# An S5 layer's tail on one core: gate stored raw, states copied by ScalarE, differences of four rows on GpSimd

## The chip, the core and the metric

One of the cores of a Trainium2 chip runs the whole kernel. TensorE (PE) does the matrix products, VectorE (DVE), ScalarE (ACT) and GpSimd (POOL) the elementwise work, and SyncE (SP) and ScalarE issue the transfers between HBM and the on-chip memory SBUF; products land in PSUM. Each engine works through its own list of instructions in a fixed order and waits on semaphores of the others. The metric is the device time of one execution in microseconds (us).

## What is computed

The reference is an encoder trunk of four layers, two with latent attention and two with an S5 state-space layer. The change touches the S5 layer, in short:

```python
u     = x @ w_u                        # 64 groups of 16 channels
s     = scan(lam, B u)                 # complex diagonal recurrence along the sequence
y     = gelu(C s + D u + ...)          # outputs of the groups, width 1024
gate  = silu(x @ w_gate)
o     = (y * sigmoid(y @ w_glu + b_glu) * gate) @ w_out
x     = layer_norm(ALPHA * x + o)
```

All of it is float32; a product is made of three matrix products of rounded parts (a high part and the difference that is left).

## The kernel before, in words

The 1536 tokens (1024 of the prompt, 512 of the sample) lie along the free dimension, the 1024 channels are eight rows of 128 partitions (row m, or kt when it is the inner dimension of a product). `mm3` (L89, L90, L91) multiplies: high by high, high weight by row difference, weight difference by high.

The S5 layer runs in overlapping stages. `states_in` (L1235 to L1239) brings the inputs of the states of eight groups at a time from PSUM to two SBUF places, SA for the first half of the groups and SB for the second. `step` (L1249, L1250) is one step of the scan on VectorE, for one of two sequences (128 and 64 chunks) of one half; `advance` deals such steps out among other work. `gate` makes passes over `x @ w_gate` on TensorE with weights streamed from HBM (WG); the last six are passes 8 to 13, two columns of 512 tokens each. At a pass's end ScalarE writes silu of each product to a buffer in R (L1356) and from there to HBM (SG2).

Between the matrix products of passes 8 to 13 come `first(0)` to `first(9)`. Each calls `states_out(i)` (L1376 on VectorE, L1377 and L1378 on ScalarE), which turns the states of four groups into the order that the next product reads and puts them in one place in X0/X3 (for i from 10 on, two places by turns), and `outputs(i)` (L1392 to L1394 on TensorE, Gelu L1396 on ScalarE), whose result goes to HBM as Y. Outputs 0 to 7 need the scan of the first half, 8 to 15 that of the second.

Then comes the glu product `y @ w_glu`. `load_y(m)` fetches a row of Y (L1438), GpSimd rounds it to the high part (L1439), VectorE takes the difference (L1440). `load_w(m)` does the same for weights (L1453 load, L1454 on ScalarE, L1455 on VectorE). Rows 0 and 1 go to X2, which the operand of the gate product holds until the last pass is done; rows 2 to 5 go to SA, which is free once the states of output 7 are copied. Weights 0 go to XN, weights 1 to X1. `early(kt)` makes the part of row kt of six products at once (six accumulators of the first two output rows), in between outputs 10 to 15. `finish` (L1468, L1471, L1473, L1474) adds the two parts of y on VectorE, multiplies by the gate on GpSimd, takes the sigmoid of the product on ScalarE, multiplies on VectorE and stores. It is called 24 times.

Names: S and B are PSUM tiles; SA, SB, XN, R and X0 to X3 are regions of SBUF (X in the profile is any of the last four). The program is written in one order and a scheduler with a timeline of its own sets the fixed order of each engine's list.

## Time and profile before

| | us |
|---|---|
| median of 3 runs (lowest, highest) | 1635.17 (1633.77, 1637.13) |
| profiled execution, whole | 1637.0 |
| its span, first to last instruction | 1635.1 |
| PE busy | 1569.0 (96%) |
| DVE busy | 1113.1 (68%) |
| ACT busy | 584.6 (36%) |
| POOL busy | 307.7 (19%) |

The mean granted clock of TensorE is 0.986 of full speed. To read the profile: the share of busy time tells which engine is close to its limit overall; the table of waits tells on what TensorE stood still and how long; the table of stretches tells where its clock fell; and the rows of time tell which instruction on which engine ended a wait.

### The profile page before, as it was taken

How to read it: one execution, taken by the hardware profiler on the slowest of the kernel's cores; microseconds unless marked ns; L12 is line 12 of the kernel's file. 1: busy time of each engine (PE TensorE's matmuls, PEld its weight loads, DVE VectorE, ACT ScalarE, POOL GpSimd, SP SyncE). 2: the span in 40 equal slices, each digit the busy share in tenths (PEclk: the TensorE clock that was granted, in tenths of full speed). 3: DMA queues.
4: the chain of work that ended last, by engine and by line, in shares of the span. 5: the costliest groups of instructions: out<-in, count | busy, mean ns of one | idle time of the engine just before them, and what ended most of it. 6: DMA issues, size and time to landing. Idle time of an engine off the chain costs nothing.

```text
span 1635.1 us, 23610 instructions
## 1 busy us (share of the span) xinstructions
PE 1569.0 (96%) x7948; PEld 1330.2 (81%) x7948; DVE 1113.1 (68%) x3077; ACT 584.6 (36%) x1025; POOL 307.7 (19%) x524
## 2 busy tenths in 40 slices
PE   7999999899999999999999999999899969999997
PEld 7997878788888888788888888887678758888886
DVE  5549992667776766888667742499489863554766
ACT  3434331344535444444511113416625425321000
POOL 6810000322223222343201000000000001333110
PEclk9999999999999999999999999999999979999999
DMA  5665566523222335533434427525687738765443
GB/s 185 170 174 188 174 224 227 169 74 90 62 81 87 103 98 172 180 105 101 156 125 130 132 74 189 159 40 155 186 255 240 238 122 253 230 193 185 146 146 89
DMA packets 205928, 249.66 MB, mean 153 GB/s; under 512 B 26608, under 2 KB 149104, under 8 KB 204784
## 3 DMA queue, kind: packets, MB, share of 16 engines
q1 hardware_dynamic: 197168, 232.36, 47.3%
q10 hardware_dynamic: 8640, 15.80, 2.6%
q8 instruction: 63, 1.03, 0.3%
q14 instruction: 57, 0.47, 0.1%
HBM read 155.89 MB, written 90.11 MB: 150 GB/s over the span
## 4 chain that ended last, share of the span: by engine, by line
PE 75%; DMA 9%; DVE 7%; ACT 3%; SPq 2%; issue 2%; POOL 1%; ACTq 0%; DVEq 0%; POOLq 0%
PE B L90 12%; PE B L89 12%; PE B L91 12%; PE S L89 8%; PE S L91 8%; PE S L90 8%; PE B L554 3%; PE S L1230 2%; PE S L520 2%; PE S L519 2%; DMA SA<-CH 1%; PE B L1393 1%; PE B L1394 1%; DMA SG<-R 1%; DMA R<-WG 1%
## 5 line engine op out<-in xcount | busy, mean ns | idle before, releaser
L89 PE MATMUL B<-X,SB 128*128 128x512 f32 x392 | 155.2, 396 | 0.0
L90 PE MATMUL B<-X,SB 128*128 128x512 f32 x392 | 154.1, 393 | 0.0
L91 PE MATMUL B<-X,SB 128*128 128x512 f32 x392 | 153.9, 393 | 0.0
L539 POOL TENSOR_SCALAR SC<-SC,R 128x1024 f32<-128x1024 f32 (+1 forms) x96 | 98.5, 1027 | 214.2 <-DVE R L538 189.7
L556 ACT CAST X<-B 128x512 fp32r<-128x512 f32 x160 | 89.5, 591 | 129.0 <-PE B L554 128.4
L557 DVE TENSOR_TENSOR X<-B,X 128x512 fp32r<-128x512 f32 x160 | 105.8, 683 | 25.3 <-ACT X L556 25.0
L532 ACT ACTIVATE SC<-S,R 128x1024 f32<-128x1024 f32 (+1 forms) x96 | 93.9, 978 | 62.9 <-DVE R L529 54.0
L529 DVE TENSOR_REDUCE R<-S 128x1 f32<-128x1024 f32 (+1 forms) x96 | 99.3, 1039 | 24.0 <-PE S L520 23.9
L554 PE MATMUL B<-ident,SC 128*128 128x128 f32 x640 | 88.7, 272 | 2.0 <-POOL SC L539 2.0
L554 PEld LDWEIGHTS B<-ident,SC 128*128 128x128 f32 x640 | 76.2, 140 | 16.2 <-POOL SC L539 2.5
L89 PE MATMUL B<-X,R 128*128 128x512 f32 x192 | 80.1, 418 | 6.7 <-DMA R<-WG 3.7
L91 PEld LDWEIGHTS B<-X,SB 128*128 128x128 f32 x392 | 74.0, 189 | 15.3
L89 PEld LDWEIGHTS B<-X,SB 128*128 128x128 f32 x392 | 74.0, 189 | 14.7
L90 PEld LDWEIGHTS B<-X,SB 128*128 128x128 f32 x392 | 74.0, 189 | 14.7
L1250 DVE TENSOR_TENSOR SB<-SB,scan 128x32 f32<-128x32 f32 (+1 forms) x504 | 80.0, 209 | 0.2 <-DMA R<-WG 0.2
L1250 DVE TENSOR_TENSOR SA<-SA,scan 128x32 f32<-128x32 f32 (+1 forms) x504 | 78.2, 212 | 0.0
L90 PE MATMUL B<-X,R 128*128 128x512 f32 x192 | 76.5, 398 | 0.0
L91 PE MATMUL B<-X,R 128*128 128x512 f32 x192 | 75.9, 395 | 0.0
L89 PE MATMUL S<-SA,X 128*128 128x384 f32 (+2 forms) x200 | 68.6, 347 | 5.7 <-POOL SA L96 5.5
L1249 DVE TENSOR_TENSOR scan<-SB,lam 128x64 f32<-128x64 f32 (+1 forms) x252 | 57.3, 260 | 21.2 <-ACT SB L1238 21.2
L90 PE MATMUL S<-SA,X 128*128 128x384 f32 (+2 forms) x200 | 68.0, 342 | 0.3 <-DVE SA L97 0.3
L91 PE MATMUL S<-SA,X 128*128 128x384 f32 (+2 forms) x200 | 68.0, 341 | 0.0
(461 smaller groups left out, 4206.7 us busy)
## 6 DMA issues: line engine op xcount, KB each, us to landing
R<-WG SPq DMA_DIRECT2D x112, 128.0 KB, 3.5
R<-EU SPq DMA_DIRECT2D x52, 224.0 KB, 3.2
EU<-SA SPq DMA_DIRECT2D x16, 512.0 KB, 3.6
WO<-SA SPq DMA_DIRECT2D x8, 1024.0 KB, 5.3
WG<-X SPq DMA_DIRECT2D x16, 512.0 KB, 3.0
X<-WO SPq DMA_DIRECT2D x16, 512.0 KB, 6.0
SG<-SC ACTq DMA_DIRECT2D x24, 256.0 KB, 3.1
SC<-SG SPq DMA_DIRECT2D x24, 256.0 KB, 2.9
```

What stands on the lines that cost most here:

```text
L89: nc.tensor.matmul(ps, ah, bh, start=first, stop=False)
L90: nc.tensor.matmul(ps, ah, bl, start=False, stop=False)
L91: nc.tensor.matmul(ps, al, bh, start=False, stop=last)
L519: nc.tensor.matmul(S[:, cs], qs[:, q], self.kr[kc][0], start=False, stop=False)
L529: nc.vector.reduce_max(nm, self.S[:, :L], axis=AX.X, negate=True)
L532: nc.scalar.activation(P, self.S[:, :L], AF.Exp, bias=nm, accum_out=rsum)
L539: nc.gpsimd.tensor_scalar(P, P, rsum, 0.0, op0=ALU.mult, op1=ALU.add)
L554: nc.tensor.transpose(ps[:, t, :], P[:, (t0 + t) * 128:(t0 + t + 1) * 128], self.k.ident)
L556: nc.scalar.copy(a[:, :, qsl], ps)
L557: nc.vector.tensor_sub(b[:, :, qsl], ps, a[:, :, qsl])
L1249: return [lambda: nc.vector.tensor_mul(t, prev.unsqueeze(2).broadcast_to(sh), lam), lambda: nc.vector.tensor_add(cur, cur, t[:, 0]), lambd ...
L1250: lambda: nc.vector.tensor_add(cur, cur, t[:, 0]), lambda: nc.vector.tensor_add(cur, cur, t[:, 1])]
```

## The change

The diff, cut to its core (line numbers of the changed kernel are one or two lower than those of the kernel before up to about L1425, and one to five higher from there to L1476):

```diff
-    nc.scalar.activation(k.bcol[:, 0:1], sg[:, 0:1], AF.Exp, scale=0.0)
...
     a.kproj(0, 1)
+    k.nc.scalar.activation(k.bcol[:, 0:1], k.gq[:, 0:1], AF.Exp, scale=0.0)
...
-    yield
-    nc.vector.tensor_scalar(s1, k1, 127.0, 8388608.0, op0=ALU.add, op1=ALU.mult)
-    nc.vector.tensor_scalar(s2, kf, 127.0, 8388608.0, op0=ALU.add, op1=ALU.mult)
+    nc.gpsimd.tensor_scalar(s1, k1, 127.0, 8388608.0, op0=ALU.add, op1=ALU.mult)
+    nc.gpsimd.tensor_scalar(s2, kf, 127.0, 8388608.0, op0=ALU.add, op1=ALU.mult)
...
-                k.xn = Region(k, "XN", (8, F32R), (4, F32))
+                k.xn = Region(k, "XN", (10, F32))
...
-            nc.scalar.activation(sg, acc[c], AF.Silu)
+            nc.scalar.copy(sg, acc[c])
...
     def states_out(i):
-        reg, at = (xb, 9) if i >= N0 and i % 2 == 0 else (xa, 25)
+        reg, at = ((k.xn, 0), (xa, 25))[i % 2]
...
-        nc.vector.tensor_copy(st[0:64], xv[0:64])
+        nc.scalar.copy(st[0:64], xv[0:64])
...
-    yat = {0: (xc, 0), 1: (xc, 12)}
+    sy = Region(k, "SA", (48, F32R))
+    yat = {m: (sy, 12 * m) for m in range(4)}
+    yat.update({4: (xc, 0), 5: (xc, 12)})
...
-        nc.vector.tensor_sub(y[:, 1], raw, y[:, 0])
+        (nc.gpsimd if m < 4 else nc.vector).tensor_sub(y[:, 1], raw, y[:, 0])
...
-        if m:
-            reg, at = gat[m % 3]
-        else:
-            reg, at = k.xn, 0
+        reg, at = gat[m % 3]
...
-            reg, at = (xb, 22 if m < 3 else (16, 12)[m % 2] + 2 * h) if m else (k.xn, 8 + 2 * h)
+            reg, at = (xb, 22 if m < 3 else (16, 12)[m % 2] + 2 * h) if m else (k.xn, 6 + 2 * h)
...
-        nc.gpsimd.tensor_mul(sg, sg, y)
         sig = xb.tile([128, 512], F32, "fsig", 8, 10, 20)
         nc.scalar.activation(sig, ps, AF.Sigmoid, bias=bcol[:, m:m + 1])
+        t = k.xn.tile([128, 512], F32, "ft", 0, 2, 4)
+        nc.scalar.activation(t, sg, AF.Sigmoid)
+        nc.vector.tensor_mul(y, y, t)
+        nc.gpsimd.tensor_mul(sg, sg, y)
```

In words: the gate's products go to HBM as they are, and `finish` makes silu of them as the product with a sigmoid, one more instruction on ScalarE and one more on VectorE in each of 24 calls. `states_out` is wholly on ScalarE, with two places by turns for all sixteen outputs. Rows 0 to 3 of y lie in SA and their differences are taken by GpSimd; rows 4 and 5 lie in X2. Weights 0 of the glu go to X2 and no longer to XN, whose place holds states (their raw parts stay in XN). An instruction that makes ScalarE hold the table for Exp moves from the end of the first phase to the start of attention, and four small integer instructions move from VectorE to GpSimd.

What this does to the order on two engines is shown below. The first piece is ScalarE's list at outputs 8 to 10 in the kernel before; SB is the place of the second half's states, B the outputs' PSUM tiles (L1377 and L1378 are copies of states, L1396 the Gelu of an output):

```order
L1377 COPY X3_10778<-SB_9622 64x8x128
L1377 COPY X1_11903<-SB_9622 64x8x128
L1396 ACT_TABLE_LOAD
L1396 ACTIVATE X0_10777<-B_11820 128x384
L1396 ACTIVATE X0_10777<-B_11828 128x384
L1377 COPY X3_10778<-SB_9622 64x8x128
L1378 COPY X3_10778<-SB_9622 64x8x64
L1396 ACTIVATE X0_10777<-B_11872 128x384
```

The same place in the changed kernel, from the last copy of a gate product (L1355) on; L1453 is the rounding of glu weights, XN_8528 and X3_10777 the two places of states:

```order
L1355 COPY R_8539<-B_11795 128x512
L1453 CAST X2_11904<-XN_8528 128x512 x2
L1453 CAST X1_11903<-X1_11902 128x512
L1356 DMA SG2_66<-R_8539 128x512
L1453 CAST X1_11903<-X1_11902 128x512
L1375 COPY XN_8528<-SB_9621 64x1536
L1376 COPY XN_8528<-SB_9621 64x8x128
L1375 COPY X3_10777<-SB_9621 64x1536
L1376 COPY X3_10777<-SB_9621 64x8x128
L1395 ACTIVATE X0_10776<-B_11819 128x384
L1395 ACTIVATE X0_10776<-B_11827 128x384
L1375 COPY XN_8528<-SB_9621 64x1536
```

The copies of the lower 64 partitions (L1375; on VectorE before, L1376 there) stand ahead of the others on ScalarE, the table load is gone, and all four roundings of weights 0 and 1 stand between the last gate product and the first copy. The next piece is VectorE's list near the end of the second half's scan in the kernel before; SB and scan2 are the scan's operands, L1440 the difference of a row of y, L1455 that of weights:

```order
L1440 TENSOR_TENSOR X2_11905<-X2_11905 128x1536
L1250 TENSOR_TENSOR SB_9622<-SB_9622,scan2_81 128x2x16 x2
L1249 TENSOR_TENSOR scan2_81<-SB_9622,lam_78 128x4x16 x2
L1250 TENSOR_TENSOR SB_9622<-SB_9622,scan2_81 128x2x16 x4
L1249 TENSOR_TENSOR scan2_81<-SB_9622,lam_78 128x4x16
L1440 TENSOR_TENSOR X2_11905<-X2_11905 128x1536
```

And near the end of that scan in the changed kernel (L1248 and L1249 are the scan's steps there, L1454 the weights' difference):

```order
L1248 TENSOR_TENSOR scan2_81<-SB_9621,lam_78 128x4x16 x2
L1454 TENSOR_TENSOR X2_11904<-XN_8528,X2_11904 128x512
L1249 TENSOR_TENSOR SB_9621<-SB_9621,scan2_81 128x2x16 x2
L1454 TENSOR_TENSOR X2_11904<-XN_8528,X2_11904 128x512
L1249 TENSOR_TENSOR SB_9621<-SB_9621,scan2_81 128x2x16 x2
L1454 TENSOR_TENSOR X1_11903<-X1_11902,X1_11903 128x512
```

Before, four differences of rows of y and two of weights 1 stand among the scan's last instructions. Now all four differences of weights stand there instead: two and two scan instructions lie between the first three, 29 between the third and the fourth, and 7 behind it, so that 40 scan instructions follow the first. The rows' four differences stand on GpSimd, each behind a rounding.

TensorE's list holds the same instructions in both kernels from the last gate product to the last instruction of output 15 (90 products 128x512 and 94 pairs 128x192), in a slightly different order.

## Rows read from the trace of the kernel before

**Rows 1.** What TensorE waited for, 1200 to 1430 us: total, count, longest.

```profile
PE S L89 <- POOL X L1439: 6.5, 1, 6.5
PE B L1393 <- ACT X L1377: 3.9, 1, 3.9
PE B L1393 <- ACT X L1378: 3.5, 1, 3.5
PE B L89 <- DMA R<-WG: 2.4, 2, 2.0
```

**Rows 2.** Stretches: busy PE, PEld, DVE, ACT, POOL (instructions), granted clock, DMA share, GB/s.

```profile
1300.00:1325.00 25.00, 16.36 (x51) 12.01 (x52) 22.00 (x115) 3.52 (x5) 5.20 (x3) 0.73 0.59 201
1325.00:1350.00 25.00, 17.64 (x71) 16.22 (x70) 12.14 (x59) 10.66 (x10) 0.00 (x0) 0.80 0.18 56
...
1425.00:1450.00 25.00, 25.00 (x112) 20.71 (x111) 15.69 (x18) 4.74 (x7) 10.36 (x7) 1.00 0.67 202
```

**Rows 3.** Rows of time, TensorE: start, duration; gate's end (next product waits), end of output 15.

```profile
1308.14 0.59 PE L1392 MATMUL B<-X 128*128 128x192 f32 x2 [1.15 <-ACT R L1356]
1315.24 0.79 PE L89 MATMUL S<-X,XN 128*128 128x512 f32 x1 [6.51 <-POOL X L1439]
...
1384.53 0.49 PE L1393 MATMUL B<-X,X 128*128 128x192 f32 x2
1384.85 0.49 PE L1394 MATMUL B<-X,X 128*128 128x192 f32 x2
```

**Rows 4.** Rows of time, VectorE: start of the second half's scan, first copies behind it.

```profile
1174.56 0.29 DVE L1249 TENSOR_TENSOR scan<-SB,lam 128x128 f32<-128x128 f32 x1 [21.17 <-ACT SB L1238]
...
1331.54 2.84 DVE L1376 COPY X<-SB 64x1536 f32<-64x1536 f32 x2
```

**Rows 5.** VectorE's groups beside the scan, 1174.5 to 1332: busy, mean ns, idle before.

```profile
L1376 DVE COPY X<-SA 64x1536 f32<-64x1536 f32 x8 | 12.4, 1552 | 6.3 <-PE B L1394 6.3
L1440 DVE TENSOR_TENSOR X<-X 128x1536 fp32r<-128x1536 f32 x2 | 3.5, 1754 | 2.0 <-POOL X L1439 2.0
L1440 DVE TENSOR_TENSOR SA<-SA 128x1536 fp32r<-128x1536 f32 x2 | 3.5, 1753 | 4.9 <-POOL SA L1439 4.9
L1455 DVE TENSOR_TENSOR X<-X,X 128x512 fp32r<-128x512 f32 x2 | 1.4, 688 | 1.0 <-ACT X L1454 1.0
```

**Rows 6.** Groups of ScalarE, 1330 to 1375 us; the last over the whole span.

```profile
L1377 ACT COPY X<-SB 64x1024 f32<-64x1024 f32 x8 | 15.6, 1963 | 12.5 <-DVE SB L1250 12.3
L1378 ACT COPY X<-SB 64x512 f32<-64x512 f32 x6 | 6.5, 1079 | 0.0
L1396 ACT ACTIVATE X<-B 128x384 f32<-128x384 f32 x13 | 6.2, 490 | 13.5 <-PE B L1394 13.4
...
L1278 ACT CAST SB<-SC 128x1024 fp32r<-128x1024 f32 x8 | 8.5, 1057 | 16.7 <-PE B L90 9.9 <-DMA SC<-in_w_u 5.7 <-PE B L91 1.0
```

**Rows 7.** Rows of time of GpSimd, then VectorE, where both work.

```profile
1304.35 1.48 POOL L1439 TENSOR_SCALAR SA<-SA 128x1536 fp32r<-128x1536 f32 x1 [11.81 <-DMA SA<-Y]
...
1303.67 0.35 DVE L1249 TENSOR_TENSOR scan<-SB,lam 128x64 f32<-128x64 f32 x2
...
1304.40 1.64 DVE L1249 TENSOR_TENSOR scan<-SB,lam 128x64 f32<-128x64 f32 x2
...
1316.89 1.55 DVE L1250 TENSOR_TENSOR SB<-SB,scan 128x32 f32<-128x32 f32 x2
```

**Rows 8.** Groups of GpSimd and VectorE in the finish stage.

```profile
L1471 POOL TENSOR_TENSOR X<-X 128x512 f32<-128x512 f32 x24 | 35.5, 1482 | 69.4 <-DMA X<-SG 69.3
...
L1474 DVE TENSOR_TENSOR X<-X 128x512 f32<-128x512 f32 x24 | 23.3, 975 | 12.5 <-POOL X L1471 11.5 <-ACT X L1473 1.0
```

**Rows 9.** DMA issues: count, KB each, median us to landing; 1405 to 1540, then 1300 to 1330.

```profile
X<-SG SPq DMA_DIRECT2D x22, 256.0 KB, 3.5
...
X<-in_w_glu SPq DMA_DIRECT2D x3, 256.0 KB, 2.5
```

**Rows 10.** The chain that ended last, at the start of attention.

```profile
292.63 1.28 ACT L315
```

More of the change, by code (lines that the diff above doesn't have):

```diff
@@ L1002, in prep_a @@
         step = ld["st"]
-        yield from exp_exact(self.k, self, step, step)
+        exp_exact(self.k, self, step, step)
         yield
@@ L1008, in prep_a @@
         cs = self.t("cs", [128, G])
-        yield from exp_exact(self.k, self, x, x)
+        exp_exact(self.k, self, x, x)
         yield
@@ L1490, in early @@
                 glu(acc[i][c], ws[i], kt, c)
-    def second_y():
-        sy = Region(k, "SA", (48, F32R))
-        yat.update({i: (sy, 12 * i - 24) for i in range(2, 6)})
     done = 0
-    second_y()
     for i in range(N0, 16):
```

## The prediction

> **What bounds the kernel now.** By the table of busy times TensorE is the busiest engine by far, so a change pays where it stands still or runs at half clock, and nowhere else. I read its waits first, for the stages that the change touches, then the stretches, then the rows of time around the longest waits. From 1200 to 1430 us there is one bad place: the glu's first product waits 6.5 us for row 0 of y, then two outputs wait 3.9 and 3.5 us for state copies [rows 1]. The stretches from 1300 and from 1325 hold only 16.36 and 17.64 us of TensorE work in 25, at a granted clock of 0.73 and 0.80; from 1425 TensorE has 25.00 of 25 [rows 2]. So after about 1400 the finish stage hides all that other engines do, and what can be gained in the S5 layer lies between the gate's end (about 1306.4: the first output product behind it starts at 1308.14 after a wait of 1.15) and the end of output 15 (1384.85 plus 0.33, so 1385.2) [rows 3].
>
> TensorE's work there is the same in both kernels: 90 products at 0.223 us (25.00 us for 112 [rows 2]) and 94 pairs at 0.325 (1384.53 to 1384.85 [rows 3]), 50.6 us in all. Before it takes 1385.2 - 1306.4 = 78.8 us, so 28 us at most are to be had. What sets the end of output 15 is a chain of two legs: the last step of the second half's scan (VectorE is through at 1331.5 [rows 4]), then the copies of states 8 to 15 and their outputs, 1385.2 - 1331.5 = 53.7 us.
>
> **First leg, the scan.** From 1174.56, when the second half may start, to 1331.54 VectorE has 157.0 us [rows 4]. Beside the scan it does 8 copies of states (12.4), 4 differences of y rows (3.5 + 3.5), 2 of weights (1.4), and it stands 6.3 + 2.0 + 4.9 + 1.0 = 14.2 us [rows 5]. That leaves 122.0 of scan. The change takes the copies, the rows and the waits ahead of them away. It puts the four weight differences into the last 40 scan instructions (order, VectorE). Six such instructions take 0.73 us (a round that begins at 1303.67, the next at 1304.40 [rows 7]), 40 take 4.8; so the first weight difference could come at 1174.6 + 122.0 - 4.8 = 1291.8.
>
> Against that stands GpSimd. While it rounded a row of y for 1.48 us at 1304.35, two scan instructions of VectorE took 1.64 instead of 0.35, and the like at 1316.89 (1.55) [rows 7]: while one works, the other stands. The change puts 4 differences of 128x1536 on GpSimd, which the trace doesn't have. From above: a product of 128x512 on GpSimd takes 1.48 with such disturbance in it [rows 8], three 4.4; from below, VectorE's own 1.75 [rows 5]. GpSimd's row is the nearer; I take 3.8. Four rows at 1.48 + 3.8 are 21.1 us in which VectorE stands, less 1.3 + 1.2 which the 122.0 hold already: 1291.8 + 18.6 = 1310.4. (The Trainium skill, GPSIMD Engine Reference, Performance versus the Vector engine, gives 4497 ns for a two-input add of 2048 columns, so an estimate of 3.4 for 1536; with it this leg would be 1.6 us shorter. No run shown so far has such an instruction.)
>
> The weights 0 now lie in X2, free only at the gate's end; I put that at 1305, since the outputs' copies ahead of it no longer wait for VectorE but the loads of three rows of y can still hold up the gate's weights as before (2.4 us [rows 1]). The rounding on ScalarE (0.6 each, between the 0.49 of 384 columns and the 1.06 of 1024 [rows 6]) is done by 1306.5, ahead of VectorE. Then: difference 0.69, scan 0.25, 0.69, 0.25, 0.69, at 1313.0. The last piece of weights 1 reuses the place of the one before: load 2.5 [rows 9], rounding 0.6, difference 0.69, 1316.8, while 29 scan instructions (3.5) go by; 7 more (0.85) end the scan at about **1318**, 13.5 us sooner than now. TensorE has its first 48 products (10.7 us) from 1311 on, to 1322.
>
> **Second leg, the state copies.** Per state ScalarE copied 64x1024 (1.96) and 64x512 (1.08) [rows 6]; it gets 64x1536 as well, which VectorE did in 1.55 [rows 5]. By the slope of the first two, 0.88 per 512, it takes 2.84 on ScalarE. That row is the right one, since it reads the same strided states; a plain rounding of 128x1024 takes 1.06 [rows 6], half of it. States 8 and 9 have their third piece done beforehand: 4.8 each. Then come, in ScalarE's order, six times two Gelus (0.98) and a whole state (5.88): 6.86. The last output takes TensorE 3.9. From the scan's end: 9.6 + 41.2 + 3.9 = 54.7, against 53.7 now. TensorE alone would need 1322 + 40 = 1362 for the rest, so this chain decides, at 1318 + 54.7 = 1372.7. Small overlaps of ScalarE's instructions and some half clock in TensorE's gaps I let cancel. Gain: 1385.2 - 1372.7 = **12.5 us**. Behind output 15 the same row loads and products follow; what TensorE does there stays.
>
> (The Trainium skill, ScalarE: Activation LUTs, What ACT_TABLE_LOAD costs, has one element a cycle, 186 ns + 0.833 per element: an estimate of 1.47 for 1536 columns. The rows of 64x1024 contradict it for these strided reads: 1.96 where it gives 1.04. By the page the time would be that of the first rival.)
>
> **The other parts.** In the gate passes ten table loads (Silu and Gelu by turns) of 1.28 each, as in [rows 10], go from ScalarE, 12.8 us; eight more copies (states 0 to 7) cost it 22.7. Two places let it work one output ahead there, with some 11 us of gate products in between, so I cost this at nothing; without that cover each state would cost a few us. In the finish stage each of 24 calls gains a sigmoid (0.6 to 0.7, as a rounding) and a product on VectorE (0.69 to 0.98 [rows 5, 8]) under 24 products of TensorE (5.36): nothing, with VectorE at 15.69 and ScalarE at 4.74 of 25 [rows 2]. At the start of attention the table load of 1.28 stands in the chain [rows 10]; moved to where ScalarE waits anyway, it gives 0 to 1.4, I take 1.0. The integer instructions are small and in the background: nothing.
>
> Sum: 1637.0 - 12.5 - 1.0 = 1623.5 for the profiled execution; the median lay 1.8 below it, so 1622.
>
> **Rivals.** (1) The forward copy runs on ScalarE at the plain rate: (1.057 - 0.490)/640 per column [rows 6], 1.5 for 1536. Then 2 x 3.5 + 6 x 5.5 + 3.9 = 44; TensorE and the chain meet at 1362, the gain is 23 + 1, time 1611. For it: forward reads, where those shown are reversed. Against it: the stride is the same. (2) GpSimd keeps VectorE from the scan longer. Each us of a difference beyond 3.8 costs four; at 6.9 the scan ends at 1330.4 and nearly all is lost: 1634, and 1630 at 6.0. For it: in the finish stage VectorE's product of 128x512 takes 0.98 on average beside GpSimd's, where 0.69 is plain [rows 5, 8]. (The Trainium skill, SBUF - State Buffer, SBUF: two separate sides, says that of a two-input instruction of VectorE and one of GpSimd the one that starts first blocks the other fully; the rows of 1.64 and 1.55 agree.) (3) Slower: the longer chain of a finish. Its gate buffer is one of two, so load, ScalarE, VectorE, GpSimd, VectorE must go round in two finishes, 10.7 us. Before: 3.5 [rows 9] + 1.48 + 0.98 = 6.0; now + 0.69 + 1.0 = 7.7, without time in each engine's queue. If the queues add more than 3.0 it decides; at 13 us each of some 18 finishes loses 1.15, 21 us in all: 1643. For it: GpSimd there already waits 69.3 us for gate loads [rows 8]. Against it: 3 us of queues each time is much for engines with a third idle.
>
> **How the numbers follow.** The forecast has 0.58, rival (1) 0.15, (2) 0.14, (3) 0.10, and 0.03 go to small losses in the gate passes. The forecast's own width, from the difference's bounds (1.75 to 4.4: -8 to +2.4 us, the low end cut off by loads at about -4) and 2 us each for gate's end and clock, is 1615 to 1629. The range takes in (1) and (2): 1609 to 1636, leaving out (3) and a little. A measurement of this kernel can tell about 0.2% or 3.3 us from no change. Faster: the forecast, (1) and half of (2), 0.80; same: half of (2) and the rest, 0.10; slower: (3), 0.10.
>
> **What would show it.** Right, if the scan's last step comes near 1318, the 64x1536 copy on ScalarE takes 2.6 to 3.0, ScalarE is busy without a gap from there to the last state, TensorE's waits there read "ACT L1375 to L1377" and the wait for the y row is gone; and if the stretches past 1400 still have TensorE at 25 of 25. Wrong, if the copy takes 1.5, if the GpSimd difference takes 6 or more, if TensorE waits for the weights' difference beyond 1312, or if a finish shows TensorE waiting on PSUM.

## The result, and the profile of the changed kernel

The changed kernel takes 1626.62 us (median of 6 runs, 1622.02 to 1628.78) against 1636.24 (6 runs, 1633.77 to 1637.36) for the kernel before beside it: a ratio of 0.9934 with a 95% interval of 0.9921 to 0.9946, so 10.8 us faster, with 8.8 to 12.9 by the interval. (The ratio is estimated from all the runs; the medians alone differ by 9.6 us.) The prediction said 1622, and a profiled execution 13.5 us below that of before; it is 12.4 below (1624.55 against 1637.0), and 12.3 by the spans (1622.8 against 1635.1). The size is close. How it is made up is not what the prediction said, and most of this part is about that.

The head of the page of the changed kernel, busy time by engine:

```profile
span 1622.8 us, 23654 instructions
PE 1565.0 (96%) x7948; PEld 1324.9 (82%) x7948; DVE 1104.4 (68%) x3077; ACT 633.2 (39%) x1056; POOL 322.7 (20%) x532
```

ScalarE has 49 us more than before and GpSimd 15, VectorE 9 less. None of that tells the time; TensorE's waits from 1200 to 1430 us do (us in total, times, longest), to be laid beside [rows 1]:

```profile
PE B L89 <- DMA R<-WG: 5.3, 2, 3.1
PE B L1392 <- ACT XN L1377: 4.8, 2, 2.5
PE B L1392 <- ACT XN L1376: 3.6, 1, 3.6
PE B L89 <- ACT R L1355: 1.1, 1, 1.1
```

The 6.5 us for row 0 of y are gone. The waits for copies of states are there as foreseen, and a bit larger. The loads of the gate's weights (WG) hold TensorE 5.3 us where it was 2.4. The stretches of 25 us that answer to [rows 2] (busy time of PE, PEld, DVE, ACT, POOL with counts, granted clock, DMA share, GB/s):

```profile
1300.00:1325.00 25.00, 20.34 (x80) 16.74 (x79) 7.83 (x44) 13.95 (x13) 2.95 (x1) 0.86 0.35 113
1325.00:1350.00 25.00, 19.37 (x93) 18.15 (x92) 1.76 (x1) 24.76 (x18) 1.47 (x1) 0.86 0.91 273
1425.00:1450.00 25.00, 25.00 (x112) 20.71 (x111) 14.42 (x20) 10.43 (x15) 6.84 (x5) 1.00 0.68 216
```

TensorE does 20.3 and 19.4 of 25 us where it did 16.4 and 17.6, at a clock of 0.86 for 0.73 and 0.80; from 1325 on ScalarE is at 24.76 of 25, the bound there. In the finish stage TensorE still has 25 of 25.

### The profile page after: what moved, and what is told of

It is laid out like the page before. It is cut to its first block, busy times and chain, and to the rows that moved or that the text cites. A ratio compares the mean times of both kernels' runs of the same rounds, so it can differ in the third digit from the quotient of the medians.

```text
span 1622.8 us, 23654 instructions
## 1 busy us (share of the span) xinstructions
PE 1565.0 (96%) x7948; PEld 1324.9 (82%) x7948; DVE 1104.4 (68%) x3077; ACT 633.2 (39%) x1056; POOL 322.7 (20%) x532
## 4 chain that ended last, share of the span: by engine, by line
PE 67%; DVE 12%; DMA 10%; ACT 5%; issue 2%; SPq 2%; POOL 1%; ACTq 0%; DVEq 0%; POOLq 0%
PE B L90 10%; PE B L89 10%; PE B L91 10%; PE S L89 8%; PE S L91 8%; PE S L90 8%; PE B L552 3%; DVE SA L1249 2%; DVE scan L1248 2%; PE S L1229 2%; PE S L518 2%; PE S L517 2%; DMA X<-SG 1%; DMA SA<-CH 1%; DMA X<-in_s_w_out 1%
## 5 line engine op out<-in xcount | busy, mean ns | idle before, releaser
L91 PEld LDWEIGHTS B<-X,SB 128*128 128x128 f32 x392 | 74.1, 189 | 15.3
L90 PEld LDWEIGHTS B<-X,SB 128*128 128x128 f32 x392 | 74.1, 189 | 14.7
L1249 DVE TENSOR_TENSOR SB<-SB,scan 128x32 f32<-128x32 f32 (+1 forms) x504 | 80.8, 213 | 0.5 <-DMA R<-WG 0.5
L1248 DVE TENSOR_TENSOR scan<-SB,lam 128x64 f32<-128x64 f32 (+1 forms) x252 | 64.9, 293 | 17.4 <-ACT SB L1237 17.4
L89 PE MATMUL S<-SA,X 128*128 128x384 f32 (+2 forms) x208 | 70.8, 345 | 5.9 <-POOL SA L96 5.4
L1249 DVE TENSOR_TENSOR SA<-SA,scan 128x32 f32<-128x32 f32 (+1 forms) x504 | 75.4, 200 | 0.0
L90 PE MATMUL S<-SA,X 128*128 128x384 f32 (+2 forms) x208 | 70.6, 341 | 0.4 <-DVE SA L97 0.4
L91 PE MATMUL S<-SA,X 128*128 128x384 f32 (+2 forms) x208 | 70.1, 339 | 0.4 <-DVE X L1454 0.4
```

Source lines behind the costliest of these rows:

```text
L89: nc.tensor.matmul(ps, ah, bh, start=first, stop=False)
L90: nc.tensor.matmul(ps, ah, bl, start=False, stop=False)
L91: nc.tensor.matmul(ps, al, bh, start=False, stop=last)
L1248: return [lambda: nc.vector.tensor_mul(t, prev.unsqueeze(2).broadcast_to(sh), lam), lambda: nc.vector.tensor_add(cur, cur, t[:, 0]), lambd ...
L1249: lambda: nc.vector.tensor_add(cur, cur, t[:, 0]), lambda: nc.vector.tensor_add(cur, cur, t[:, 1])]
```

## The landmarks that all kernels share

Most executions of one kernel lie within some 5 us of its median, single ones up to 9 off, so a single span doesn't settle small differences. The stages inside an execution do better. The table gives for the profiled execution of every kernel: the start of the gate's first product, the gate's end (the start of the first output product behind the gate's last one; in before 1306.40, and the 1308.14 of [rows 3] is the next pair, which waits 1.15 us for ScalarE), the end of the scan's last instruction on VectorE, the end of output 15, and the span; then the two stages that follow, and the ratio of times to the kernel before. Times in us, all read from rows of time of the kernel named.

| kernel | gate begins | gate ends | scan end | output 15 | span | gate's end to output 15 | behind it | ratio (95%) |
|---|---|---|---|---|---|---|---|---|
| before | 1104.4 | 1306.4 | 1331.6 | 1385.2 | 1635.1 | 78.8 | 249.9 | 1 |
| after | 1097.2 | 1300.6 | 1313.2 | 1370.4 | 1622.8 | 69.8 | 252.4 | 0.9934 (0.9921 to 0.9946) |
| b_early | 1097.7 | 1299.3 | 1324.6 | 1379.7 | 1630.3 | 80.4 | 250.6 | 0.9964 (0.9947 to 0.9981) |
| u_exp | 1104.5 | 1304.6 | 1316.9 | 1373.0 | 1625.4 | 68.3 | 252.4 | 0.9938 (0.9918 to 0.9958) |
| u_table | 1102.0 | 1307.4 | 1319.8 | 1375.7 | 1628.6 | 68.3 | 252.9 | 0.9957 (0.9942 to 0.9972) |
| g_silu | 1097.7 | 1305.0 | 1317.5 | 1374.6 | 1625.9 | 69.6 | 251.3 | 0.9963 (0.9950 to 0.9976) |
| e_ydve | 1098.0 | 1298.7 | 1316.8 | 1372.8 | 1627.2 | 74.1 | 254.4 | 0.9943 (0.9924 to 0.9962) |
| d_wpool | 1095.8 | 1300.8 | 1296.8 | 1363.1 | 1618.6 | 62.4 | 255.5 | 0.9899 (0.9878 to 0.9920) |
| c_dve8 | 1096.3 | 1297.0 | 1309.3 | 1358.5 | 1611.0 | 61.5 | 252.5 | 0.9864 (0.9843 to 0.9884) |
| h_both | 1097.7 | 1301.7 | 1298.8 | 1362.3 | 1614.4 | 60.6 | 252.1 | 0.9855 (0.9833 to 0.9877) |
| m_w1raw | 1100.6 | 1303.7 | 1300.9 | 1365.2 | 1617.2 | 61.5 | 252.0 | 0.9876 (0.9855 to 0.9897) |
| w_part | 1105.5 | 1306.7 | 1319.5 | 1375.3 | 1627.7 | 68.5 | 252.4 | 0.9917 (0.9893 to 0.9941) |
| p_yact | 1098.0 | 1299.9 | 1312.4 | 1362.6 | 1615.2 | 62.8 | 252.6 | 0.9850 (0.9832 to 0.9869) |
| r_dveall | 1096.2 | 1299.5 | 1323.4 | 1372.5 | 1625.1 | 73.0 | 252.6 | 0.9937 (0.9923 to 0.9950) |

Read the column "gate's end to output 15" first: the four kernels with the S5 tail of after (after, u_exp, u_table and, but for its shorter loads, w_part) have 68.3 to 69.8, the two with the tail of before 78.8 and 80.4. So the tail itself gained 9 to 12 us in this stage. The column "gate ends" scatters by 10 us among kernels with the same early part, so the lead with which an execution arrives there (5.8 us in after) is known worse.

The column "gate begins" tells where that lead comes from. The first products of the gate in before, after and b_early:

```profile
1104.44 0.53 PE L89 MATMUL B<-X,R 128*128 128x512 f32 x1
```

```profile
1097.24 0.53 PE L89 MATMUL B<-X,R 128*128 128x512 f32 x1
```

```profile
1097.73 0.53 PE L89 MATMUL B<-X,R 128*128 128x512 f32 x1
```

After is 7.2 us ahead there, before the gate has done anything, and b_early, which has the early edits alone, 6.7. Of the eleven kernels with both early edits ten begin the gate between 1095.8 and 1100.6; the eleventh, w_part, begins it at 1105.5. From the gate's first product to its end after takes 203.4 us and before 202.0.

## Experiments

Each kernel is the changed one with the edit shown, unless another is named. A difference of two kernels is the difference of their ratios, times 1636 us, with the half widths of both intervals combined as the root of the sum of squares. An error in the ratio of after itself would shift all comparisons with it alike.

### Is the scan or the copying the bound: weight differences of rows 0 and 1 to GpSimd (d_wpool)

```diff
-            nc.vector.tensor_sub(w[:, 1, hs], raw, w[:, 0, hs])
+            (nc.gpsimd if m < 2 else nc.vector).tensor_sub(w[:, 1, hs], raw, w[:, 0, hs])
```

> The changed kernel with the differences of the glu's weights 0 and 1 on GpSimd, so that nothing that waits for the gate's end stands among the last 40 scan instructions. Account B: VectorE no longer stands 9.4 us for the gate's end nor 3.0 for the second load of weights 1; the scan ends near 1298 to 1300 instead of 1313, ScalarE's first copy of a state begins behind its roundings at about 1303 to 1304, output 15 ends near 1362 instead of 1370.4, time 1617 to 1621. Rival: the scan's end was not what the outputs waited for (the glu's 48 products and the gate's end were), then at most 3 us are won, 1623 to 1627; or GpSimd's slower weight differences delay the 48 products by more than the 1.2 us each that they take, and it is slower.

Why VectorE is late in after is seen in its rows of time (start, duration, engine, line, out<-in, and in brackets the idle time ahead with its releaser):

```profile
1278.68 3.68 DVE L1248 TENSOR_TENSOR scan<-SB,lam 128x64 f32<-128x64 f32 x2
1282.28 3.05 DVE L1249 TENSOR_TENSOR SB<-SB,scan 128x32 f32<-128x32 f32 x4
1285.26 6.92 DVE L1248 TENSOR_TENSOR scan<-SB,lam 128x64 f32<-128x64 f32 x2
...
1302.29 1.20 DVE L1454 TENSOR_TENSOR X<-XN,X 128x512 fp32r<-128x512 f32 x1 [9.39 <-ACT X L1453]
...
1304.43 0.68 DVE L1454 TENSOR_TENSOR X<-X,X 128x512 fp32r<-128x512 f32 x1
...
1311.65 0.69 DVE L1454 TENSOR_TENSOR X<-X,X 128x512 fp32r<-128x512 f32 x1 [3.04 <-ACT X L1453]
```

The first weight difference stands in VectorE's list ahead of the last scan steps, and its input is rounded only at the gate's end, from 1301.64 on, behind ScalarE's last copy of a gate product. VectorE got there at 1292.9 and stood 9.39 us with scan steps behind it, and 3.04 for the second piece of weights 1. With these differences on GpSimd the scan ended at 1296.8, 16.4 us sooner. Output 15 came only 7.3 sooner, and the whole time 5.7 us (1.7 to 9.7), as account B had it. ScalarE took the first state late, since its list has the gate's last copies and the roundings ahead:

```profile
1302.81 0.61 ACT L1453 CAST X<-X 128x512 fp32r<-128x512 f32 x1
1303.33 2.99 ACT L1375 COPY XN<-SB 64x1536 f32<-64x1536 f32 x1
```

From there to output 15 it is 59.8 us, near the 57.3 that after takes from its scan's end. So the head-of-line wait is real and costs what ScalarE can make up of it, but the copies set the pace behind.

### The copies of states 8 to 15 back on VectorE (c_dve8)

```diff
-        nc.scalar.copy(st[0:64], xv[0:64])
+        (nc.vector.tensor_copy if i >= 8 else nc.scalar.copy)(st[0:64], xv[0:64])
```

> The changed kernel with the lower halves of states 8 to 15 copied by VectorE again, nothing else. Account A and B alike: the chain of copies behind the scan (57.3 us from the scan's end to output 15) loses 2.8 us a state on ScalarE; TensorE's waits for state copies there (9.3 us in all) go, the scan's end stays at about 1313. Output 15 ends at 1362 to 1364 instead of 1370.4, time 1619 to 1621. Rival: the products of outputs are then held by their operands' loads, and only 3 us are won.

In after, ScalarE's copies between 1311 and 1366 us (count, busy us, mean ns, idle ahead):

```profile
L1375 ACT COPY XN<-SB 64x1536 f32<-64x1536 f32 x4 | 11.5, 2867 | 1.5 <-DVE SB L1249 1.5
L1375 ACT COPY X<-SB 64x1536 f32<-64x1536 f32 x4 | 11.4, 2860 | 0.1
L1376 ACT COPY X<-SB 64x1024 f32<-64x1024 f32 x4 | 7.9, 1969 | 0.1
```

and in c_dve8 the same copies on VectorE, between 1309 and 1366:

```profile
L1375 DVE COPY XN<-SB 64x1536 f32<-64x1536 f32 x4 | 6.1, 1526 | 14.3 <-PE B L1393 14.3
L1375 DVE COPY X<-SB 64x1536 f32<-64x1536 f32 x4 | 6.1, 1520 | 7.8 <-PE B L1393 7.8
```

ScalarE copies with hardly a gap, 2.87 us a piece. VectorE takes half of that, and in c_dve8 waits for TensorE, not the other way round. TensorE's waits from 1200 to 1430 in c_dve8:

```profile
PE B L89 <- DMA R<-WG: 3.7, 3, 2.2
PE S L91 <- DVE X L1454: 2.8, 1, 2.8
PE B L1392 <- DMA X<-WO: 1.9, 1, 1.9
PE B L1391 <- ACT R L1355: 0.4, 1, 0.4
```

No wait for a copy is left, and the gain over after is 11.5 us (7.5 to 15.4), more than expected; in the profiles 8.3 of it lie between the gate's end and output 15. This half of the edit, on its own, was a loss of that size inside a change that gained.

### Both (h_both)

The edit of c_dve8 on d_wpool.

> As the kernel with weight differences 0 and 1 on GpSimd, and the lower halves of states 8 to 15 copied by VectorE again (states 0 to 7 stay on ScalarE, two places as changed). Account B: both legs are cut. Per output ScalarE has 3.0 + 0.9 us in place of 6.7, below TensorE's 3.9 to 5, so from the gate's end TensorE is held only by its own work: 1301.7 + 50.6 + 3 to 5 us of waits, output 15 ends near 1356 to 1358, time 1611 to 1615. Rival: what holds the outputs is the loads of their operands or the gate's weights, then it is no faster than the kernel with the weight differences alone.

Ratio 0.9855, not to be told from c_dve8 alone (1.5 us, -3.4 to 6.4). The scan ends at 1298.8, 10.5 us before that of c_dve8, and nothing comes of it: once the copies are fast, neither leg of the chain holds TensorE. From the gate's end to output 15 it is 60.6 and 61.5 us, of which TensorE is busy 54.3 and 55.7, beside the 50.6 us of work at full clock that the prediction counted; its longest waits there are for a difference of weights (2.5 and 2.8) and a load of WO (1.8 and 1.9).

### All copies on VectorE (r_dveall, on c_dve8)

```diff
-        (nc.vector.tensor_copy if i >= 8 else nc.scalar.copy)(st[0:64], xv[0:64])
+        nc.vector.tensor_copy(st[0:64], xv[0:64])
```

> The changed kernel with the lower halves of all sixteen states copied by VectorE again, two places as changed. Account A: eight more copies of 1.55 us ahead of the scan's end, 12.4 us, against the run with states 8 to 15 alone on VectorE (1616.3): about 1625 or more. Account B: VectorE stands 6 to 9 us ahead of the gate's end anyway, so at most 3 to 6 of the 12.4 us are seen: 1618 to 1622. So the copies of states 0 to 7 on ScalarE are worth 2 to 6 us, those of states 8 to 15 cost about 10.

12 us slower than c_dve8 (7.9 to 15.9) and level with after, so account A was right. Eight copies take 12.4 us on VectorE before the scan is through (by VectorE's groups from 1163 to 1324 us), and now VectorE arrives late at the weights, at 1309.12 without a wait. TensorE's longest wait, and the rows of VectorE:

```profile
PE S L91 <- DVE X L1454: 7.9, 1, 7.9
```

```profile
1309.12 0.69 DVE L1454 TENSOR_TENSOR X<-XN,X 128x512 fp32r<-128x512 f32 x1
...
1323.39 1.45 DVE L1375 COPY XN<-SB 64x1536 f32<-64x1536 f32 x1
```

So, both taken against c_dve8, the two halves of the edit go opposite ways. States 0 to 7 on ScalarE pay 12 us, since VectorE is the bound while the scan runs; states 8 to 15 there cost 11.5, since ScalarE is the bound after it. Together they come to about nothing.

### The differences of y back on VectorE (e_ydve)

```diff
-        (nc.gpsimd if m < 4 else nc.vector).tensor_sub(y[:, 1], raw, y[:, 0])
+        nc.vector.tensor_sub(y[:, 1], raw, y[:, 0])
```

> The changed kernel with all differences of rows of y back on VectorE, rows 0 to 3 staying in the first half's place. The differences of rows 0 to 2 took GpSimd 3.5 us each while VectorE stood, but behind them VectorE stood another 9.4 us for the weights' rounding, that is for the gate's end. Account A: the scan's end sets the end, so (3.5 - 1.75) x 4 = 7 us are won, about 1619 to 1621. Account B: the time falls into the 9.4 us in which VectorE stands anyway, so the scan's last step stays at about 1313 and the time at 1626 +- 1.5.

1.5 us slower than after, with -2.2 to 5.2: not resolved, but the 7 us of account A are out. The rows of GpSimd in after and of VectorE in e_ydve, both of the stretch from 1270 on:

```profile
L1442 POOL TENSOR_TENSOR SA<-SA 128x1536 fp32r<-128x1536 f32 x4 | 14.0, 3504 | 0.2
```

```profile
L1442 DVE TENSOR_TENSOR SA<-SA 128x1536 fp32r<-128x1536 f32 x4 | 7.0, 1755 | 18.4 <-POOL SA L1440 18.4
```

On GpSimd a difference takes twice as long, and VectorE stands meanwhile: the two scan instructions of 3.68 and the two of 6.92 us, shown above, run beside one and beside two differences of GpSimd, the second of these here:

```profile
1285.16 6.94 POOL L1442 TENSOR_TENSOR SA<-SA 128x1536 fp32r<-128x1536 f32 x2
```

On VectorE it is short, but stands in the list ahead of scan steps and waits there for the rounding by GpSimd, 18.4 us in all, 16.7 of them for row 0, whose rounding itself waits for its load. The stage from the gate's end to output 15 is 74.1 us for 69.8, the scan's end 3.6 later; the whole time shows less than that.

### The integer instructions of the exponential back on VectorE (u_exp), and both early edits alone (b_early)

u_exp:

```diff
+    yield
-    nc.gpsimd.tensor_scalar(s1, k1, 127.0, 8388608.0, op0=ALU.add, op1=ALU.mult)
-    nc.gpsimd.tensor_scalar(s2, kf, 127.0, 8388608.0, op0=ALU.add, op1=ALU.mult)
+    nc.vector.tensor_scalar(s1, k1, 127.0, 8388608.0, op0=ALU.add, op1=ALU.mult)
+    nc.vector.tensor_scalar(s2, kf, 127.0, 8388608.0, op0=ALU.add, op1=ALU.mult)
...
-        exp_exact(self.k, self, step, step)
+        yield from exp_exact(self.k, self, step, step)
```

> The changed kernel with the four integer instructions of exp_exact back on VectorE and its yields back; all else as changed. Account A (the prediction's): these are small and in the background, so nothing moves, 1626.6 +- 1. Account B (read from the two traces): the changed kernel is 3.6 us ahead of the kernel before already at the first product of L1105 (138.9 against 142.6), because TensorE's waits for the activation L217 fell from 5.1 to 2.9 us and its clock there no longer fell; then taking the edit back costs 3 to 4 us, 1629.5 to 1631, with a wait for L217 of about 5 us again.

b_early is the kernel before with the same lines turned the other way round, and with the Exp instruction at the start of attention; nothing of the S5 tail.

> The kernel before with the two small edits ahead of the S5 layer alone: the integer instructions of exp_exact on GpSimd without their yields, and the instruction that loads the table for Exp moved to the start of attention. Account A (the prediction's): 1.0 us for the table and nothing for the integers, 1635.5 to 1636. Account B (from the traces): the first product of L1105 comes near 138 instead of 142.6 and the inputs of the states near 993 instead of 999.4; if all of it lasts to the end, 1629 to 1631; if the S5 layer's tail takes part of it back, as the run with the integers taken back suggests (8 us ahead at the scan's start, 2.6 at the end), 1632 to 1634.

The waits of TensorE between 20 and 420 us in after and in u_exp, first lines:

```profile
PE B L236 <- ACT SC L217: 2.9, 2, 2.1
```

```profile
PE B L236 <- ACT SC L217: 5.9, 2, 3.5
```

Before has 5.1 in this line, b_early 2.9. The first product of L1105 (L1104 where the yield is gone) starts at 142.57 in before, 143.09 in u_exp, 138.93 in after and 137.37 in b_early. So the early edits do give some 4 to 5 us at 140 us. By the whole time b_early is 5.9 us faster than before (3.1 to 8.7). But u_exp is only 0.7 us slower than after (-3.2 to 4.5): undone in the new kernel, what the same lines cost is not resolved, and the interval still holds 4 us. Its profile arrives 7.3 us later than after's at the gate's first product and 4.0 later at its end, and has 68.3 us from there to output 15, where after has 69.8. A lead that is in part given back in the tail would do that; so would scatter. These runs don't tell the two apart.

### The table of the exponential back at the end of the first phase (u_table)

```diff
+    nc.scalar.activation(k.bcol[:, 0:1], sg[:, 0:1], AF.Exp, scale=0.0)
...
-    k.nc.scalar.activation(k.bcol[:, 0:1], k.gq[:, 0:1], AF.Exp, scale=0.0)
```

> The changed kernel with the instruction that loads the table for Exp back at the end of the first phase. Account A: 1.0 us. Account B: the wait for the difference L482 at the start of attention goes from 1.1 back to 2.6 us, in all 1.3 to 1.5 us up to there, of which the tail may take back a part: 1627 to 1628.5.

The wait at the start of attention that the edit was to shorten, in u_table and in after:

```profile
PE B L89 <- DVE X L484: 2.6, 1, 2.6
```

```profile
PE B L89 <- DVE X L482: 1.1, 1, 1.1
```

1.5 us of it are direct. The whole time is 3.8 us longer than after's (0.6 to 7.0). The interval holds the 1.5 of the wait; if there is more, I found no row for it.

### Silu back in the gate passes and out of the finish (g_silu)

```diff
-            nc.scalar.copy(sg, acc[c])
+            nc.scalar.activation(sg, acc[c], AF.Silu)
...
-        t = k.xn.tile([128, 512], F32, "ft", 0, 2, 4)
-        nc.scalar.activation(t, sg, AF.Sigmoid)
-        nc.vector.tensor_mul(y, y, t)
```

> The changed kernel with silu back in the gate stage and out of the finishes. Account A: nothing moves, 1626.6 +- 1. Account B: the stretch behind output 15 was 249.9 and 250.6 us in the kernels without this part and 252.0 to 255.5 in those with it, so 2 us are won back there; the ten table loads come back on ScalarE ahead of it, which cost 0 to 2 us in the gate passes and in front of the outputs. Sum 1624.5 to 1627.

4.7 us slower than after (1.8 to 7.7), which neither account had: the raw gate pays, where the prediction had costed it at nothing. ScalarE's groups from 1160 to 1311 us in g_silu show the tables back:

```profile
L1395 ACT ACT_TABLE_LOAD x4 | 5.1, 1283 | 2.8 <-DMA R<-WG 2.7
L1355 ACT ACT_TABLE_LOAD x4 | 5.1, 1283 | 0.1
```

In after there is one, of 1.3 us. But the traces don't show how these loads would cost TensorE its time. From 1200 to 1283 us, where most of them lie, TensorE doesn't wait longer for ScalarE's release of a gate product (L1355) in g_silu than in after, first the line of g_silu:

```profile
PE B L1391 <- ACT R L1355: 0.9, 2, 0.5
```

```profile
PE B L89 <- ACT R L1355: 1.1, 1, 1.1
```

The difference of waits that I find lies ahead of the first of them, at 1212: from 1160 to 1200 TensorE waits 4.2 us for gate weights in g_silu (2.0 in after). Its gate takes 207.3 us from its first product to its end, against 200.1 to 205.4 in the kernels with the raw gate, and the scan ends 4.3 us later than in after; but before and b_early, with silu in the gate, have 202.0 and 201.5. So the 4.7 us are shown by the whole time alone, and their cause is not.

Behind output 15 g_silu has 251.3 us, against 252.0 to 255.5 for all kernels with silu in the finish and 249.9 and 250.6 for the two without the change there. So the finish does seem to pay something for silu, some 1 to 2 us by these single profiles, and the whole kernel gets more than that back.

### Do the loads of rows of y delay the gate's weights (w_part, p_yact, m_w1raw)

In w_part rows 0 to 2 of y are loaded in their first 512 columns alone, which stand in for the other columns, so that part of the output is another, and GpSimd does its work on them in pieces of 512.

```diff
-        nc.sync.dma_start(raw, k.Y[m])
+        if m < 3:
+            nc.sync.dma_start(raw[:, 0:512], k.Y[m, :, 0:512])
...
+        else:
+            nc.sync.dma_start(raw, k.Y[m])
```

> The changed kernel with rows 0 to 2 of y loaded in their first 512 of 1536 columns only (these stand in for the other columns too; GpSimd's work stays, in pieces of 512). It tests what holds the gate's weights near 1284 and 1293, for 2.2 and 3.1 us. Account B: the three loads of 768 KB that the change brings ahead of the gate's end; with a third of their bytes these waits fall below 2 us in all and the gate ends 3 to 4 us sooner (about 137.5 to 139 us behind the last product of the states' inputs instead of 142). Rival: the weights are late for their place in R, or for the outputs' own loads and stores, and the two waits stay.

The waits for gate weights from 1200 us on fell from 5.3 to 3.7. In after there are two, 45 and 24 products ahead of the gate's last:

```profile
1284.54 0.50 PE L89 MATMUL B<-X,R 128*128 128x512 f32 x1 [2.22 <-DMA R<-WG]
1293.38 0.80 PE L89 MATMUL B<-X,R 128*128 128x512 f32 x1 [3.11 <-DMA R<-WG]
```

In w_part the first is gone (a wait of 0.7 lies at 1200), and the second stayed:

```profile
1299.38 0.50 PE L89 MATMUL B<-X,R 128*128 128x512 f32 x1 [3.04 <-DMA R<-WG]
```

What SyncE had in hand ahead of that one, in w_part (issues of transfers, in order):

```profile
1288.81 6.67 SPq L1399 DMA_DIRECT2D Y<-X  x8
1295.58 2.20 SPq L1324 DMA_DIRECT2D R<-WG  x4
```

Eight stores of an output row took SyncE 6.7 us to issue, and the gate's weights stand behind them. So half of the theory held: the weights for the first wait come in time when the three loads ahead of them have 256 KB each and not 768. The second wait is left to the rival, the stores that are issued ahead. The time, 2.8 us below after (-1.6 to 7.2), is not resolved. p_yact takes those eight stores from SyncE, on c_dve8:

```diff
-                nc.sync.dma_start(k.Y[m].rearrange("(g p) (j c) -> j p g c", p=16, j=8)[j], y[j * 16:(j + 1) * 16])
+                (nc.scalar if m == 3 else nc.sync).dma_start(k.Y[m].rearrange("(g p) (j c) -> j p g c", p=16, j=8)[j], y[j * 16:(j + 1) * 16])
```

> The changed kernel with the lower halves of states 8 to 15 on VectorE again, and with the eight stores of outputs 6 and 7 (row 3 of Y) issued by ScalarE and no longer by SyncE. In the changed kernel SyncE was busy from 1282.9 to 1289.3 with these eight issues, and the gate weights that stand behind them in its list were issued at 1289.4 and landed 3.1 us late. Account B: that wait goes, the gate ends 2 to 3 us sooner, 1612.5 to 1615 against 1616.3 without this edit. Rival: the weights are late for the rows of y on the same DMA engines, then nothing moves, 1616.3 +- 1.5; or ScalarE's eight issues hold back its copies of gate products, then slower.

The second wait, 24 products ahead of the gate's last and 1.2 to 3.3 us long in all eleven other kernels with the new tail, is gone: the weights for it were issued at 1287.12. What is left is the first wait, 45 products ahead, which w_part's shorter loads had taken away and which is 0.8 to 2.6 us long in the others:

```profile
1287.10 0.50 PE L89 MATMUL B<-X,R 128*128 128x512 f32 x1 [2.61 <-DMA R<-WG]
```

So the two waits have two causes: the loads of three rows of y for the first, the issuing of eight stores for the second. At 1611.09 us p_yact has the best median of all, and 2.3 us below c_dve8 by the ratios (-2.2 to 6.8), so not shown to be better. m_w1raw gives the second raw piece of weights 1 a place of its own, on h_both, so that its load need not wait for the piece before:

```diff
-            reg, at = (xb, 22 if m < 3 else (16, 12)[m % 2] + 2 * h) if m else (k.xn, 6 + 2 * h)
+            reg, at = (xb, (22, 9)[m == 1 and h] if m < 3 else (16, 12)[m % 2] + 2 * h) if m else (k.xn, 6 + 2 * h)
```

> The kernel with weight differences 0 and 1 on GpSimd and the copies of states 8 to 15 on VectorE, and now with a place of its own (free since the states left it) for the second raw piece of weights 1, so that its load needn't wait for the first piece's difference. In the run without it that load landed at about 1312.7, 10 us behind the gate's end. If the first outputs or the glu's last products wait for it, 1 to 3 us are won, 1611 to 1614; if TensorE never waited for it (its trace shows only 2.5 us of wait for a GpSimd difference, that of weights 0), nothing moves, 1614.8 +- 1.5.

Ratio 0.9876 against 0.9855 (3.4 us slower, -1.5 to 8.4): no gain. TensorE waits 2.5 us once for a difference of weights on GpSimd (L1454), as in h_both, and for no later piece.

## Point by point

**TensorE and the bound: right.** Its work between the gate and output 15 was put at 50.6 us and the rest called waits. The stage went from 78.8 to 69.8, and to 61.5 with the copies of states 8 to 15 moved back. TensorE is busy 60.0 of the 78.8 and 59.5 of the 69.8 us, at a mean clock of 0.87 and 0.90, so nearly all of the gain there is waiting that is gone.

**First leg, the scan: near by its end, wrong by its reason.** The scan was to end 13.0 us behind the gate's end, put at 1305. The gate ends at 1300.6, and the scan ends 12.5 us later. Within it the GpSimd difference took 3.50 us (taken: 3.8), and VectorE stood with it, as 6.92 us for two scan instructions show. By the Trainium skill, GPSIMD Engine Reference, Performance versus the Vector engine, the estimate was 3.4, and the trace agrees better with it than with mine. What I did not see: VectorE was ready for the weights at 1292.9 and stood 12.4 us for their roundings, with scan steps queued behind. The step that failed is "1291.8 + 18.6 = 1310.4", which let VectorE come to them after the roundings of 1306.5. It came 17.5 us sooner than that: 11.0 since the scan began at 1163.61 and not at 1174.56, and the remaining 6.5 mostly since the fourth row (its rounding begins at 1297.93, its difference at 1299.49, 1.48 and 3.46 us) fell into the time in which VectorE stood and held no scan step up. So the lead of 11 us with which the scan began came to nothing, as weights and gate set its end. With VectorE waiting for the roundings, the third weights' difference ended 4.5 us behind the gate's end (1304.43 + 0.68) and not 8.0. A second term was too small by about as much: the load of the last piece of weights 1, issued at 1305.13, took 5.8 us and not 2.5, and ScalarE, whose rounding stands ahead of the last difference, waited for it:

```profile
1310.99 0.62 ACT L1453 CAST X<-X 128x512 fp32r<-128x512 f32 x1 [7.69 <-DMA X<-in_w_glu]
```

That 12.5 came out for 13.0 is luck: the two errors, 3.5 and 3.3 us, took each other away.

**Second leg, the copies: right.** 2.87 us a copy for 2.84; 57.3 us from the scan's end to output 15 for 54.7; ScalarE nearly without a gap (24.76 of 25 us from 1325 on), TensorE waiting for L1376 and L1377. The Trainium skill, ScalarE: Activation LUTs, What ACT_TABLE_LOAD costs, gives an estimate of 1.47 us, by which rival (1) would have come. The trace doesn't agree: this strided copy takes 2.87, and rival (1), which needed 1.5, falls with it. What I did not draw from it: with VectorE copying at 1.53 us, c_dve8 has 49.2 us in this leg. The prediction had both durations (2.84 and 1.55 [rows 5]) and had ScalarE as the bound of the leg, and still counted the 1 us to the old leg's 53.7 as the cost of the move; it did not ask what the leg would be with the new order and the copies left where they were.

**Gate's end: mis-sized.** Put 1.4 us sooner (1305 for 1306.4); it came 5.8 us sooner in the profile. The lead is not made in the gate: it is 7.2 us at the gate's first product, and b_early, with the early edits alone, has 6.7 there and is 5.9 us faster as a whole. So as far as these profiles tell its source is the early edits, costed at 1.0 for the table and 0 for the integers; how they share it is not resolved. From its first product to its end the changed gate takes 1.4 us more than that of before. The raw gate, costed at 0 since two places were to let ScalarE work one output ahead, is worth 4.7 by the whole time of g_silu (1.8 to 7.7), with no row that shows where. Against it, the waits for gate weights from 1200 us on grew from 2.4 to 5.3: the one behind the loads of three rows of y, 2.2, is new, and the last one is 3.1 where it was 2.0; I had kept 2.4.

**Finish: nearly right.** I costed 0; the stage behind output 15 is 252.4 us for 249.9, and 251.3 with silu taken out of it. So 1 to 2 us by single profiles, and no sign of the 21 us of rival (3): TensorE has 25.00 of 25 in it, and VectorE's new product takes 720 ns:

```profile
L1475 DVE TENSOR_TENSOR X<-X,XN 128x512 f32<-128x512 f32 x24 | 17.2, 720 | 19.5 <-ACT XN L1474 19.4
L1476 POOL TENSOR_TENSOR X<-X 128x512 f32<-128x512 f32 x24 | 35.1, 1466 | 72.9 <-DVE X L1475 72.9
L1474 ACT ACTIVATE XN<-X 128x512 f32<-128x512 f32 x24 | 15.0, 630 | 27.1 <-DMA X<-SG 26.9
```

**Rival (2)** fell by its price, 3.50 where it needed 6.

**The sum.** Predicted: 12.5 in the tail and 1.0 at attention. Measured in the profiles: 5.8 ahead of the gate's end (7.2 ahead of its first product, -1.4 in it), 9.0 from there to output 15, -2.5 behind, 12.3 in all. By single edits undone or done alone: early edits 5.9 (b_early), raw gate 4.7 (g_silu), y differences not resolved (e_ydve), states on ScalarE +12 and -11.5. Single edits needn't add up, since each was tried in the presence of other work; that the sum is near 10.8 is not a proof. Nor does any run part what gains in the tail: with all copies back on VectorE (r_dveall) the kernel is as fast as after, so it is not the move of the copies as a whole. What is left are the rows of y in SA, the weights 0 in X2 and the two places by turns, which no run takes back. The wait of 6.5 us for row 0 of y, which is gone, points at the first of these, but that is not shown. The sign follows from the tail, as forecast. That the size came out is in part luck: the early edits, put at 1.0 in all, made up for a tail that gained 9.0 us, and not 11.1, from the gate's end on, and for the 2.5 behind output 15.

Open: what undoing the integers costs in the new kernel, whose profile begins the gate 7.3 us later and is 2.6 us longer as a whole; by what way the raw gate pays; which of the edits left in all runs makes the tail shorter; and where the rest of u_table's 3.8 us lies.

## What to carry to other kernels

Cost a moved instruction in each stage by the engine that is the bound there: the same copy was worth 12 us off VectorE while the scan ran and cost 11.5 us on ScalarE after it, and splitting the move at that point gave 0.986 where the whole gave 0.993. When an engine's list is changed, work out when the engine arrives at each instruction that waits, not only when its input comes: what stands behind a wait in the list pays for it. And before a lead is put down to the stage at whose end it is seen, look where it begins: the 5.8 us at the gate's end were there, and 1.4 more, at its first product.

## What the runs showed of the hardware

- A copy of 64x1536 from the strided states takes 2.87 us on ScalarE and 1.53 on VectorE; 64x1024 takes 1.97 on ScalarE. A rounding of a plain 128x512 on ScalarE takes 0.62.
- While GpSimd takes a two-operand difference of 128x1536 (3.50 us), VectorE's list hardly moves: two scan instructions took 6.92 us beside two differences, and four took 3.05 beside two roundings (2.95), where a round of six takes 0.73 [rows 7].
- Eight stores of 96 KB kept SyncE's list for 6.7 us in w_part, and the loads of gate weights behind them were issued only then (1295.58); with the stores issued by ScalarE the wait that followed, 2.2 us in c_dve8, is gone in p_yact.
